# Start addresses of slots, weight units and value tiles, and the job turn of the adaLN sums, in a two-block transformer kernel

## The chip, the cores and the metric

One core of a Trainium2 chip runs the whole program. The metric is the device time of one execution in microseconds (us); three runs of the kernel before were timed.

## The reference

Two blocks work on one sequence of 512 tokens with 1024 features, two layers each, all in float32. A layer of the first block takes a vector `c` to six rows of 1024 numbers, the adaLN shift, scale and gate (`silu(c) @ w_ada + b_ada`), applies them around a mixer (mLSTM heads beside dilated attention) and a SwiGLU, and normalises. The second block does the same with its own adaLN weights, a linear recurrence and stick-breaking attention in its first layer, windowed attention in its second, and a gated feed-forward with a short convolution.

```python
ada = (c_act @ w_ada[l] + b_ada[l])[:, None, :]
sh1, sc1, g1, sh2, sc2, g2 = jnp.split(ada, 6, axis=-1)
u = h * (1.0 + sc1) + sh1
y = mixer(u, w_in[l], ...)                    # u @ w_in, mLSTM, attention, @ w_out
h = layer_norm(DN_ALPHA * h + g1 * y, ...)
u = h * (1.0 + sc2) + sh2
y = (jax.nn.silu(u @ w1) * (u @ w3)) @ w2
```

## The kernel before

**Data.** Activations lie feature by partition: a tile of 128 partitions by 512 tokens in float32 (2048 bytes of each partition) is a *slot*, and there are 60 of them. A product in full precision is made of three fp32r matmuls: each operand is split into a rounded part `h` and a rest `l`, and `h*h`, `l*h` and `h*l` are accumulated in one PSUM tile. Activations are split into two slots; weights stream from HBM in chunks of 16 blocks of 128x128 (`wt`, 1 MB), which ScalarE rounds into `wh` (L517) and VectorE subtracts into `wl` (L520), in *units* of 8 blocks (4096 bytes of each partition; five units of each kind).

**Matmuls.** A matmul has a stationary operand, loaded by a LDWEIGHTS of its own, and a moving operand that streams through. `proj` (L532 to L534) streams 512 tokens of a slot past a block of `wh`, `wh`, `wl`; `proj_halves` (L577, L580, L581) does so with 256 tokens; `fetch`/`begin` (L595 to L597) and `first_block` (L1295 to L1297) are again 512 wide. `proj_tokens` (L553, L556, L557) has it the other way round: a piece of a slot is stationary and 256 columns of `wh` or `wl` are moving. In the mLSTM heads both operands are slots (L889 to L891), and L918 to L920 stream the value tiles `vn0`, `vn1` (258 columns for each of four token groups) past slots. All these are fp32r. Others, L1426 and L714 among them, take plain float32 operands and appear as two records each.

**Addresses.** Pools lie behind each other in SBUF in the order in which they are opened, and a pool's tiles in the order of their first use, each rounded up to 32 bytes: `cp` (constants, columns, `vn`), `wtp` (`wt`), `whp` (units), `adp` (`wada`), `sm` (small columns, each name with 4 buffers unless told otherwise), then `slots`. In the compiled program of before, `vn0` begins at byte 26400 of each partition, `vn1` at 30528, the first unit at 51040 and the first slot at 106400; the rest of units and slots follow in steps of 4096 and 2048. So every slot begins 416 bytes behind a multiple of 512, every unit 352 bytes behind one, and both 32 bytes behind a multiple of 64. A block within a unit and a group of 128 tokens within a slot lie a multiple of 512 bytes further on. The last slot ends 96 bytes below the end of the memory that a partition has.

**adaLN jobs.** `ada` (from L689) is a generator that runs between other work. For each group of 2048 outputs it makes four accumulators: each takes four DMAs of 512 KB (`wada`, on SP's queue, two buffers) and eight VectorE operations (L706 and the line before it). After the first, second and third it yields; after the fourth it goes on at once to four float32 matmuls that add up the 128 partitions of each accumulator (L714) and yields; in its next turn it copies, transposes (L722), adds the bias and yields a last time: five turns for a group. Turns are called by `background()` ahead of a projection: 14 in a mixer (the mixer of layer 0 has two groups to do) and 18 in each feed-forward (three groups, in three of the four); `finish_jobs()` runs what is left. There are 11 groups.

**Order around the start.** `setup` issues the loads of `vecs` (SP) and `cst` (ACT), small memsets on POOL (L642 to L683), and VectorE operations on them, of which L685 fills two columns of each `vn` from a column that POOL has set.

Of the kernel before, what the change touches and what calls it, by code (L numbers as in the profile page):

```python
# [10 lines left out]
F32 = mybir.dt.float32  # L11
F32R = mybir.dt.float32r
# [4 lines left out]
P = 128  # L17
# [434 lines left out]
class Model:  # L452
    def __init__(self, ctx, tc, ins, out, dbg=None, stop=None):
        self.tc, self.nc, self.ins, self.out, self.dbg_out, self.stop = tc, tc.nc, ins, out, dbg, stop
        self.plan = []
        pool = lambda name, bufs, **kw: ctx.enter_context(tc.tile_pool(name=name, bufs=bufs, **kw))
        self.cp = pool("cp", 1)
        self.wtp = pool("wtp", 2)
        self.whp = pool("whp", 5)
        self.adp = pool("adp", 2)  # L460
        self.drp = pool("drp", 2, space=bass.MemoryType.DRAM)
        self.sm = pool("sm", 4)
        self.pacc = pool("pacc", 3, space=PSUM)
        self.pss = pool("pss", 2, space=PSUM)
        self.pst = pool("pst", 1, space=PSUM)
        self.pso = pool("pso", 2, space=PSUM)
        self.slots = pool("slots", 1)
        self.freeq = deque(range(NSLOT))
        self.peak = NSLOT
        self.late = []  # L470
        self.flip = 0
        self.ready = {}
        self.jobs = deque()
        self.later = []


    def get(self, rounded=False):
# [150 lines left out]
    def setup(self):  # L628
        nc = self.nc
        self.vecs = self.cp.tile([P, NVEC], F32, name="vecs")  # L630
        nc.sync.dma_start(out=self.vecs, in_=self.ins["vecs"])
        n = CST["ident"]
        self.sums = self.cp.tile([P, n], F32, name="sums")
        nc.scalar.dma_start(out=self.sums, in_=self.ins["cst"][:, 0:n])
        self.x = [self.get() for _ in range(KD)]
        for k in range(KD):
            (nc.sync if k % 2 else nc.scalar).dma_start(out=self.x[k].f, in_=self.ins["xT"][k])
        self.consts = self.cp.tile([P, NCST - n], F32, name="consts")
        nc.scalar.dma_start(out=self.consts, in_=self.ins["cst"][:, n:])
        self.ident = self.cst("ident")  # L640
        self.eps = self.cp.tile([P, 2], F32, name="eps")
        nc.gpsimd.memset(self.eps[:, 0:1], LN_EPS)  # L642
        nc.gpsimd.memset(self.eps[:, 1:2], RMS_EPS)
        zero = self.cp.tile([P, 1], F32, name="zero")
        nc.gpsimd.memset(zero, 0.0)
        self.zero = zero.to_broadcast([P, T])
        self.mhalf = self.cp.tile([P, 4], F32, name="mhalf")
        nc.gpsimd.memset(self.mhalf, -0.5)
        self.ident_r = self.cp.tile([P, 128], F32R, name="ident_r")
        nc.vector.tensor_copy(self.ident_r, self.ident)  # L650
        self.csil = self.cp.tile([P, 16], F32, name="csil")
        c = self.vec("c1", 0, 16)
        th = self.small(16, "th_c")
        nc.scalar.activation(th, c, AF.Tanh, scale=0.5)
        nc.vector.tensor_scalar(out=th, in0=th, scalar1=0.5, scalar2=0.5, op0=ALU.mult, op1=ALU.add)
        nc.vector.tensor_mul(self.csil, th, c)
        self.n2sp = self.softplus_cols()
        self.n4sp = self.cp.tile([P, 4], F32, name="n4sp")
        nc.vector.tensor_scalar(out=self.n4sp, in0=self.n2sp, scalar1=2.0, scalar2=None, op0=ALU.mult)

        for l in range(DEPTH):
            for name, n in ((f"conv_w{l}_0", 96), (f"gn_w{l}", 8), (f"fcw{l}_0", 4 * KF)):
                v = self.vec(name, 0, n)
                nc.vector.tensor_scalar(out=v, in0=v, scalar1=0.5, scalar2=None, op0=ALU.mult)
        for name in ("eba", "ebx"):
            v = self.vec(name, 0, 4)
            nc.vector.tensor_scalar(out=v, in0=v, scalar1=0.5, scalar2=None, op0=ALU.mult)
        for name in ("eqg", "okg"):
            v = self.vec(name)
            nc.vector.tensor_scalar(out=v, in0=v, scalar1=0.125, scalar2=None, op0=ALU.mult)  # L670
        v = self.vec("b_ada0", 8, 8)
        nc.vector.tensor_scalar(out=v, in0=v, scalar1=1.0, scalar2=None, op0=ALU.add)
        self.dup = self.cp.tile([P, 1], F32, name="dup")
        nc.gpsimd.memset(self.dup, 1.0 / 32)
        self.adac = {}
        for blk in range(2):
            for l in range(DEPTH):
                self.adac[blk, l] = self.cp.tile([P, 48], F32, name=f"ada{blk}{l}")

        self.vn = [self.cp.tile([P, 4, 258], F32R, name=f"vn{k}") for k in range(2)]  # L680
        for k in range(2):
            col = self.small(4, "vcol")
            nc.gpsimd.memset(col, (1 - k) / 16.0)  # L683
            for j in (256, 257):
                nc.vector.tensor_copy(self.vn[k][:, :, j], col)  # L685


    def ada(self, blk, l, groups):
        nc = self.nc  # L689
        w = self.ins["ada1" if blk == 0 else "ada2"][l]  # L690
        bias = f"b_ada{l}" if blk == 0 else f"ada_b{l}"
        ad = self.adac[blk, l]
        for g in groups:
            accs = []
            for n in range(4):
                acc = self.get()
                for q in range(4):
                    wt = self.adp.tile([P, 2, T], F32, name="wada")
                    nc.sync.dma_start(out=wt, in_=w[4 * g + n, q])
                    for j in range(2):  # L700
                        k = 2 * q + j
                        c = self.csil[:, 8 * blk + k:8 * blk + k + 1]
                        if k == 0:
                            nc.vector.tensor_scalar(out=acc.f, in0=wt[:, j, :], scalar1=c, scalar2=None, op0=ALU.mult)
                        else:
                            nc.vector.scalar_tensor_tensor(out=acc.f, in0=wt[:, j, :], scalar=c, in1=acc.f,  # L706
                                                           op0=ALU.mult, op1=ALU.add)
                accs.append(acc)
                if n < 3:
                    yield  # L710

            rows = self.pss.tile([P, T], F32, name="s")
            for n, acc in enumerate(accs):
                nc.tensor.matmul(rows[32 * n:32 * n + 32, :], self.cst("ones", 32), acc.f, start=True, stop=True,  # L714
                                 tile_position=(0, 32 * n))
            self.put(accs)
            rs = self.get()
            yield
            nc.scalar.copy(rs.f, rows)
            cols = self.pst.tile([P, T], F32, name="t")  # L720
            for c in range(4):
                nc.tensor.transpose(cols[:, c * P:(c + 1) * P], rs.f[:, c * P:(c + 1) * P], self.ident)  # L722
            c0 = 16 * g
            nc.vector.tensor_tensor(out=ad[:, c0:c0 + 16].rearrange("p (n c) -> p n c", n=4),
                                    in0=cols.rearrange("p (c n e) -> p n c e", c=4, n=4)[:, :, :, 0],
                                    in1=self.vec(bias, c0, 16).rearrange("p (n c) -> p n c", n=4), op=ALU.add)

            sc = ad[:, 8:16] if g == 0 else ad[:, 32:40]
            if g != 1:
                nc.vector.tensor_scalar(out=sc, in0=sc, scalar1=1.0, scalar2=None, op0=ALU.add)  # L730
            if blk == 0 and g != 0:
                gt = ad[:, 16:24] if g == 1 else ad[:, 40:48]
                nc.vector.tensor_scalar(out=gt, in0=gt, scalar1=0.5, scalar2=None, op0=ALU.mult)
            self.put(rs)
            yield
# [51 lines left out]

    def load_rsqrt(self, dep):

        t = self.small(1, "arsd")  # L790
        return self.nc.scalar.activation(t, dep, AF.Abs_reciprocal_sqrt, bias=1.0, scale=0.0)


# [179 lines left out]
    def attention_pair(self, l, sp, u):  # L973
# [62 lines left out]
        o0 = self.pso.tile([P, T], F32, name="o")  # L1036
        o12 = self.pso.tile([P, T], F32, name="o")
        self.lastmm = {}
        ls, mx = self.small(16, "att_l"), self.small(16, "att_m")
        cols = lambda ap, x, i: ap.rearrange("p (x y i) -> p x y i", x=2, y=2)[:, x, :, i]  # L1040
        bts = [self.get(), self.get()]
        for x in range(2):
# [1 line left out]
        for i in (0, 3, 1, 2):  # L1044
# [12 lines left out]
            for x in range(2):  # L1057
# [17 lines left out]
                t = self.pst.tile([P, T], F32, name="t")  # L1075
# [36 lines left out]
        t = self.pst.tile([P, T], F32, name="t")  # L1112
# [646 lines left out]
```

## Time and profile before

| what | value |
|---|---|
| median of three runs | 3487.23 us (3484.3 to 3487.62) |
| the profiled execution's own time | 3485.64 us |
| its span, first to last instruction | 3483.8 us |
| TensorE busy, matmuls | 3407.2 us, 98% |
| VectorE busy | 2146.2 us, 62% |
| ScalarE busy | 1457.3 us, 42% |
| GpSimd busy | 186.7 us, 5% |
| mean granted TensorE clock | 0.993 |
| mean DMA rate | 114 GB/s |

PE is TensorE's matmuls, PEld its weight loads, DVE is VectorE, ACT ScalarE, POOL GpSimd, SP the sync engine that issues most DMAs. The profiled execution lasts 1.84 us longer than its span; it is 1.59 us shorter than the median. The matmul records overlap, since one is still in the array when the next starts: how fast they follow each other is read from their starts, not from their durations.

### The profile page before, as it was taken

How to read it: one execution, taken by the hardware profiler on the slowest of the kernel's cores; microseconds unless marked ns; L12 is line 12 of the kernel's file. 1: busy time of each engine (PE TensorE's matmuls, PEld its weight loads, DVE VectorE, ACT ScalarE, POOL GpSimd, SP SyncE). 2: the span in 40 equal slices, each digit the busy share in tenths (PEclk: the TensorE clock that was granted, in tenths of full speed). 3: DMA queues.
4: the chain of work that ended last, by engine and by line, in shares of the span. 5: the costliest groups of instructions: out<-in, count | busy, mean ns of one | idle time of the engine just before them, and what ended most of it. 6: DMA issues, size and time to landing. Idle time of an engine off the chain costs nothing.

```text
span 3483.8 us, 45252 instructions
## 1 busy us (share of the span) xinstructions
PE 3407.2 (98%) x17777; PEld 2786.8 (80%) x17777; DVE 2146.2 (62%) x4043; ACT 1457.3 (42%) x2558; POOL 186.7 (5%) x252
## 2 busy tenths in 40 slices
PE   7999999999999999999999999989999999999999
PEld 5788777778888888877788888877688888897887
DVE  5875545648663687554535856368888565865353
ACT  4543555225222554355523422246753234753231
POOL 1110110010000011011000000001000000000000
PEclk9999999999999999999999999999999999999999
DMA  5222222635552222222222555211146432122222
GB/s 218 91 78 80 79 79 103 220 119 178 209 184 94 75 89 79 91 73 76 78 103 85 194 186 193 97 67 61 37 140 235 163 115 85 49 73 97 97 97 73
DMA packets 76117, 395.72 MB, mean 114 GB/s; under 512 B 9200, under 2 KB 10480, under 8 KB 42496
## 3 DMA queue, kind: packets, MB, share of 16 engines
q1 hardware_dynamic: 69408, 377.90, 30.5%
q0 software_dynamic: 4480, 12.69, 1.2%
q8 instruction: 140, 2.29, 0.3%
q10 hardware_dynamic: 2016, 2.25, 0.2%
q14 instruction: 73, 0.60, 0.1%
HBM read 390.60 MB, written 2.20 MB: 113 GB/s over the span
## 4 chain that ended last, share of the span: by engine, by line
PE 84%; DVE 7%; ACT 2%; DMA 2%; issue 1%; POOL 0%; DVEq 0%; ACTq 0%; POOLq 0%
PE acc L532 21%; PE acc L534 21%; PE acc L533 21%; PE acc L577 2%; PE acc L580 2%; PE acc L581 2%; DMA wada<-in_ada_dram 1%; PE o L1096 1%; PE o L1511 1%; DVE wl L520 1%; PE s L1060 1%; DVE slot L706 1%; PE acc L553 1%; PE acc L556 1%; PE acc L557 1%
## 5 line engine op out<-in xcount | busy, mean ns | idle before, releaser
L532 PE MATMUL acc<-slot,wh 128*128 128x512 f32 x3461 | 1373.6, 397 | 14.3 <-DVE slot L802 9.0
L534 PE MATMUL acc<-slot,wl 128*128 128x512 f32 x3461 | 1365.4, 394 | 0.0
L533 PE MATMUL acc<-slot,wh 128*128 128x512 f32 x3461 | 1363.5, 394 | 0.0
L517 ACT CAST wh<-wt 128x1024 fp32r<-128x1024 f32 x522 | 547.2, 1049 | 1223.3 <-PE acc L533 1005.3
L520 DVE TENSOR_TENSOR wl<-wt,wh 128x1024 fp32r<-128x1024 f32 x522 | 645.5, 1238 | 529.4 <-ACT wh L517 520.7
L532 PEld LDWEIGHTS acc<-slot,wh 128*128 128x128 f32 x3461 | 652.6, 189 | 164.7 <-ACT wh L517 13.8
L534 PEld LDWEIGHTS acc<-slot,wl 128*128 128x128 f32 x3461 | 652.1, 188 | 144.1 <-issue 4.6
L533 PEld LDWEIGHTS acc<-slot,wh 128*128 128x128 f32 x3461 | 652.6, 189 | 142.6 <-issue 5.1
L706 DVE SCALAR_TENSOR_TENSOR slot<-wada,csil,slot 128x512 f32<-128x512 f32 x308 | 231.9, 753 | 75.3 <-DMA wada<-in_ada_dram 70.0
L577 PE MATMUL acc<-slot,wh 128*128 128x256 f32 x726 | 207.1, 287 | 4.2 <-ACT slot L376 4.2
L580 PE MATMUL acc<-slot,wh 128*128 128x256 f32 x726 | 205.7, 283 | 0.0
L581 PE MATMUL acc<-slot,wl 128*128 128x256 f32 x726 | 204.4, 282 | 0.1
L608 ACT CAST slot<-slot 128x512 fp32r<-128x512 f32 x204 | 125.4, 620 | 182.1 <-DVE slot L1260 52.8
L1194 DVE SCALAR_TENSOR_TENSOR slot<-acc,ada,slot 128x512 f32<-128x512 f32 (+1 forms) x109 | 70.1, 646 | 160.8 <-PE acc L534 120.8
L802 DVE SCALAR_TENSOR_TENSOR slot<-acc,vecs,slot 128x510 f32<-128x510 f32 (+2 forms) x217 | 159.8, 745 | 8.2 <-ACT slot L797 5.6
L609 DVE TENSOR_TENSOR slot<-slot,slot 128x512 fp32r<-128x512 f32 x204 | 144.4, 714 | 32.7 <-ACT slot L608 23.2
L577 PEld LDWEIGHTS acc<-slot,wh 128*128 128x128 f32 x726 | 136.7, 189 | 12.4 <-issue 6.2
L580 PEld LDWEIGHTS acc<-slot,wh 128*128 128x128 f32 x726 | 137.4, 189 | 2.8 <-issue 1.6
L581 PEld LDWEIGHTS acc<-slot,wl 128*128 128x128 f32 x726 | 137.3, 189 | 0.7 <-DVE wl L520 0.3
L553 PE MATMUL acc<-wh,slot 128*128 128x256 f32 x288 | 81.3, 282 | 0.0
L556 PE MATMUL acc<-wh,slot 128*128 128x256 f32 x288 | 81.2, 282 | 0.0
L557 PE MATMUL acc<-wl,slot 128*128 128x256 f32 x288 | 80.7, 280 | 0.0
(357 smaller groups left out, 3931.4 us busy)
## 6 DMA issues: line engine op xcount, KB each, us to landing
wt<-in_ws_dram SPq DMA_DIRECT2D x261, 1024.0 KB, 4.8
wada<-in_ada_dram SPq DMA_DIRECT2D x176, 512.0 KB, 4.5
slot<-in_ada_dram SPq DMA_DIRECT2D x32, 256.0 KB, 6.1
slot<-drc POOLq DMA_DIRECT2D x16, 256.0 KB, 3.6
slot<-in_bias_dram POOLq DMA_DIRECT2D x16, 256.0 KB, 2.9
slot<-dr POOLq DMA_DIRECT2D x32, 128.0 KB, 3.1
out_dram<-slot SPq DMA_DIRECT2D x8, 256.0 KB, 2.0
slot<-in_xT_dram ACTq DMA_DIRECT2D x4, 256.0 KB, 5.6
```

Of the source, the lines that this page charges most:

```text
L517: copy = nc.scalar.copy(self.wh, src)
L520: nc.vector.tensor_tensor(out=self.wl, in0=src, in1=self.wh, op=ALU.subtract)
L532: nc.tensor.matmul(acc, wh, xs[k].h.r, start=k == 0, stop=False)
L533: nc.tensor.matmul(acc, wh, xs[k].l.r, start=False, stop=False)
L534: nc.tensor.matmul(acc, wl, xs[k].h.r, start=False, stop=k == n - 1)
L577: m = nc.tensor.matmul(acc[:, hs], wh, xs[k].h.r[:, hs], start=k == 0, stop=False)
L580: nc.tensor.matmul(acc[:, hs], wh, xs[k].l.r[:, hs], start=False, stop=False)
L581: last[a] = nc.tensor.matmul(acc[:, hs], wl, xs[k].h.r[:, hs], start=False, stop=k == n - 1)
L608: copy = self.nc.scalar.copy(pair.h.r, src)
L609: self.nc.vector.tensor_tensor(out=pair.l.r, in0=src, in1=pair.h.f, op=ALU.subtract)
L706: nc.vector.scalar_tensor_tensor(out=acc.f, in0=wt[:, j, :], scalar=c, in1=acc.f, op0=ALU.mult, op1=ALU.add)
L802: nc.vector.scalar_tensor_tensor(out=out[:, lo:hi], in0=acc[:, lo + d:hi + d], scalar=w, in1=out[:, lo:hi], op0=ALU.mult, op1=ALU.add)
```

## The change

A new method `pad(pool, n)` allocates a tile of `n` bytes and sets its first element with a POOL memset. It is called five times, ahead of `sums`, ahead of `ident_r`, ahead of each `vn` tile (32 bytes each) and behind the second (96 bytes). Small tiles that had four buffers get one (`th_c`, `vcol`, `arsd`) or two (`att_l`, `att_m`). By the sizes of the tiles, `vn0` then begins at byte 26496 and `vn1` at 30656 (multiples of 64), the first unit at 51264 (64 bytes behind a multiple of 512) and the first slot at 105984 (a multiple of 512). In `ada` the generator yields after the fourth accumulator too: the four matmuls of L714 go out one turn later, and a group takes six turns.

```diff
+    def pad(self, pool, n):
+        self.pads += 1
+        t = pool.tile([P, n // 4], F32, name=f"pad{self.pads}", tag=f"pad{self.pads}", bufs=1)
+        self.nc.gpsimd.memset(t[:, 0:1], 0.0)
...
+        self.pad(self.cp, 32)
         self.sums = self.cp.tile([P, n], F32, name="sums")
...
+        self.pad(self.cp, 32)
         self.ident_r = self.cp.tile([P, 128], F32R, name="ident_r")
...
-        th = self.small(16, "th_c")
+        th = self.small(16, "th_c", 1)
...
-        self.vn = [self.cp.tile([P, 4, 258], F32R, name=f"vn{k}") for k in range(2)]
+        self.vn = []
         for k in range(2):
-            col = self.small(4, "vcol")
+            self.pad(self.cp, 32)
+            self.vn.append(self.cp.tile([P, 4, 258], F32R, name=f"vn{k}"))
+        self.pad(self.cp, 96)
+        for k in range(2):
+            col = self.small(4, "vcol", 1)
...
                 accs.append(acc)
-                if n < 3:
-                    yield
+                yield
...
-        t = self.small(1, "arsd")
+        t = self.small(1, "arsd", 1)
...
-        ls, mx = self.small(16, "att_l"), self.small(16, "att_m")
+        ls, mx = self.small(16, "att_l", 2), self.small(16, "att_m", 2)
```

## Rows read from the trace of the kernel before

**Rows 1.** The chain of waits: shares of the span by engine, then by line.

```profile
PE 84%; DVE 7%; ACT 2%; DMA 2%; issue 1%; POOL 0%; DVEq 0%; ACTq 0%; POOLq 0%
...
by line: PE acc L532 21.4%; PE acc L534 21.3%; PE acc L533 21.2%; PE acc L577 1.7%; PE acc L580 1.6%; PE acc L581 1.6%; DMA wada<-in_ada_dram 1.3%; PE o L1096 1.0%; PE o L1511 0.9%; issue 0.9%; DVE wl L520 0.9%; PE s L1060 0.8%; DVE slot L7
```

**Rows 2.** Stretches: length, busy us by engine (x count), PE clock, DMA share, GB/s.

```profile
3200.00:3300.00 100.00, 100.00 (x438) 82.07 (x437) 41.71 (x47) 27.03 (x31) 0.00 (x0) 1.00 0.27 95
```

**Rows 3.** Timeline of PE, L532 to L534, first and last of 714: start, duration.

```profile
1724.91 0.39 PE L534 MATMUL acc<-slot,wl 128*128 128x512 f32 x1
...
1888.11 0.39 PE L534 MATMUL acc<-slot,wl 128*128 128x512 f32 x1
```

**Rows 4.** Timeline of PE, L889 to L891, first and last of 12.

```profile
277.39 0.39 PE L889 MATMUL s<-slot,slot 128*128 128x512 f32 x1
...
279.88 0.39 PE L891 MATMUL s<-slot,slot 128*128 128x512 f32 x1
```

**Rows 5.** Timeline of PE, L577 to L581: ends of 120 matmuls, then of 190.

```profile
769.19 0.28 PE L577 MATMUL acc<-slot,wh 128*128 128x256 f32 x1
...
782.67 0.28 PE L581 MATMUL o<-slot,wl 128*128 128x256 f32 x1
...
809.04 0.28 PE L581 MATMUL acc<-slot,wl 128*128 128x256 f32 x1
...
831.30 0.28 PE L581 MATMUL o<-slot,wl 128*128 128x256 f32 x1
```

**Rows 6.** Timeline of PE, L553 to L557: ends of 91 matmuls, then of 96.

```profile
148.71 0.28 PE L557 MATMUL acc<-wl,slot 128*128 128x256 f32 x1
...
158.91 0.28 PE L557 MATMUL acc<-wl,slot 128*128 128x256 f32 x1
...
266.08 0.28 PE L553 MATMUL acc<-wh,slot 128*128 128x256 f32 x1
...
277.27 0.28 PE L557 MATMUL acc<-wl,slot 128*128 128x256 f32 x1
```

**Rows 7.** Timeline of PE, L532 to L534 near the start, first and last of 11.

```profile
104.58 0.40 PE L534 MATMUL acc<-slot,wl 128*128 128x512 f32 x1
...
106.91 0.39 PE L532 MATMUL acc<-slot,wh 128*128 128x512 f32 x1
```

**Rows 8.** Groups by line and shape: count, busy us, mean ns, idle before; PE's timeline, L1426.

```profile
L532 PE MATMUL acc<-slot,wh 128*128 128x512 f32 x3461 | 1373.6, 397 | 14.3 <-DVE slot L802 9.0 <-DVE slot L1259 3.3 <-ACT slot L608 1.1
...
L577 PE MATMUL acc<-slot,wh 128*128 128x256 f32 x726 | 207.1, 287 | 4.2 <-ACT slot L376 4.2
...
L553 PE MATMUL acc<-wh,slot 128*128 128x256 f32 x288 | 81.3, 282 | 0.0
...
L577 PE MATMUL o<-slot,wh 128*128 128x256 f32 x224 | 63.2, 282 | 0.0
...
L1426 PE MATMUL s<-slot,slot 128*128 128x512 f32 x16 | 7.5, 592 | 0.0
...
2356.04 1.88 PE L1426 MATMUL s<-slot,slot 128*128 128x512 f32 x4
```

**Rows 9.** Groups by line: adaLN's VectorE operations and the four sums.

```profile
L706 DVE SCALAR_TENSOR_TENSOR slot<-wada,csil,slot 128x512 f32<-128x512 f32 x308 | 231.9, 753 | 75.3 <-DMA wada<-in_ada_dram 70.0
...
L714 PE MATMUL s<-slot,sums 128*32 128x512 f32 x88 | 17.9, 605 | 5.9 <-DVE slot L706 5.9
```

**Rows 10.** Timeline of the start, POOL and DVE; idle time before in brackets.

```profile
0.90 0.13 POOL L683 MEMSET vcol<- 128x4 f32 x2
1.03 0.38 DVE L685 CAST vn<-vcol 128x4 fp32r<-128x4 f32 x4 [1.03 <-POOL vcol L683]
...
4.46 0.71 DVE L664 TENSOR_SCALAR vecs<-vecs 128x96 f32<-128x96 f32 x6 [3.04 <-DMA vecs<-in_vecs_dram]
```

**Rows 11.** Stretches with the most VectorE work, columns as in rows 2.

```profile
800.00:900.00 100.00, 98.64 (x557) 83.46 (x557) 85.10 (x133) 41.67 (x64) 0.00 (x0) 1.00 0.62 216
...
2600.00:2700.00 100.00, 100.00 (x441) 81.18 (x440) 85.52 (x119) 35.34 (x45) 0.00 (x0) 1.00 0.67 237
```

More of the change, by code (lines that the diff above doesn't have):

```diff
@@ L474, in __init__ @@
         self.later = []
+        self.pads = 0
+    def pad(self, pool, n):
+        self.pads += 1
+        t = pool.tile([P, n // 4], F32, name=f"pad{self.pads}", tag=f"pad{self.pads}", bufs=1)
+        self.nc.gpsimd.memset(t[:, 0:1], 0.0)
     def get(self, rounded=False):
```

## The prediction

> **What bounds the kernel now.** I read the chain of waits first: TensorE's matmuls hold 84% of it, and three lines, L532 to L534, hold 21.4 + 21.3 + 21.2 = 63.9% [rows 1], 2226 us of the span of 3483.8. L577, L580 and L581 hold another 4.9%, 171 us. Then the stretches: where nothing but 512-wide matmuls runs, 438 start in 100 us at a granted clock of 1.00, the level of 2.4 GHz [rows 2]. So the question is what sets the distance between two starts, the pitch.
>
> Timelines give it closely. L532 to L534 make 713 steps in 163.20 us: 228.9 ns, or 549.3 ticks of 2.4 GHz for 512 columns [rows 3]. That is 37.3 ticks over one column a tick (213.3 ns), 112 in three matmuls. L889 to L891, as wide, make 11 steps in 2.49 us, 226.4 ns, about 32 ticks over [rows 4]. The 256-wide lines run at either of two pitches: L577 to L581 at 13.48 us / 119 = 113.3 ns in one stretch and 22.26 us / 189 = 117.8 ns in another [rows 5], L553 to L557 at 10.20 / 90 = 113.3 and 11.19 / 95 = 117.8 [rows 6]. Against 106.7 ns that is 16 and 26.7 ticks over, 48 or 80 in three matmuls. Near the start, L532 to L534 even show 2.33 us / 10 = 233 ns, 48 ticks over [rows 7]. Every excess, over three matmuls, is a multiple of 16 ticks, and 16 columns of float32 are 64 bytes of a partition.
>
> So I read the excess as 64-byte pieces (6.67 ns each) that the moving operand reads, or waits for, beyond its own. The moving operands of all these lines begin 32 bytes behind a multiple of 64: they touch 33 pieces where 32 would hold the data, or 17 where 16 would. That is one extra piece in each matmul, and the whole excess of the faster 256-wide stretches. The rest, 1.33 pieces in L532 to L534, one in L889 to L891, none or 0.67 in the 256-wide lines, goes with the relation of the two operands: the weights begin 64 bytes below the moving operand (modulo 512) in L532 and L577, at the same place in L889, 64 above it in L553. I take it for meetings with the weight load that runs beside each matmul. With the weights above, six of L553's nine stretches run at the faster pitch; with the weights below, two of the ten long stretches (over 100 steps) of L577 do.
>
> **The change part by part.** *Addresses.* Slots move to multiples of 512 and units 64 bytes above: moving operands begin on a piece, a weight block fills 8 pieces instead of touching 9, and in L532 and L577 the weights come to lie 64 bytes above the moving operand, the relation that L553 has now (L553 takes the opposite one). No fp32r row has a start at a multiple of 64 with 256 or 512 columns, so the pitch is bounded from both sides: 228.9 ns if nothing changes, 213.3 if every column takes its tick and nothing else. Plain float32 matmuls, which move half a column a tick, show what is left where reading does not bind: four records of L1426 take 1.88 us and one takes 0.592, so they step at 1.288 / 3 = 429.3 ns, 2.6 over the 426.7 of 1024 ticks [rows 8]. I take that: 215.9 for 512 columns and 109.3 for 256. Both sources of excess are then gone; the second, because L553's faster stretches show it at zero under the relation that comes.
> - 512 wide: 2226 us / 228.9 ns = 9725 matmuls on the path, x 13.0 ns = 126.4 us.
> - 256 wide: 171 us / 117.3 ns (mostly the slower pitch) = 1458, x 8.0 = 11.7 us. L553 to L557 (3 x 288, [rows 8]), on average (6 x 113.3 + 3 x 117.8) / 9 = 114.8, x 5.5 = 4.8 us.
> - Were every matmul counted, on the path or not (3 x 3461 and 3 x (726 + 224), [rows 8]): 10383 x 13.0 + 2850 x 8.0 + 4.8 = 163 us. With nothing changed: 0.
>
> L532 and L889, both 512 wide at the same start, step differently [rows 3, 4], so the weight load seems to cost reading time. "TensorE: Matmul & The Clock Gate", section "Step-by-step: what each phase is for", of the Trainium skill says that the engine reads moving operand and weights through two independent ports and that loading the next weights takes nothing from the running matmul. By that rule only the extra piece could go, and the sum would be that of rival 1; by the rows it is the one above.
>
> The value tiles (480 matmuls of L918 to L920) have 258 columns, 1032 bytes, which touch 17 pieces from either start: 0, with bounds of 3 us either way (480 x 6.67). Whether VectorE, ScalarE or DMAs work faster or slower at the new addresses no row shows. They hold 11% of the chain; 2% of that is 8 us either way, and I take 0.
>
> *The four sums, a turn later.* PE waited 5.9 us in all for the last L706 ahead of L714 [rows 9]. One turn later, the eight VectorE operations (8 x 0.75 = 6 us) have a projection's time to finish, at least 24 matmuls or 5.2 us and mostly twice that. Of 5.9 us I take 4; bounds 0 and 12, twice the row, for the loads that wait along with their matmuls. The count of DMAs and operations stays. What moves: each later group's `wada` loads stand a turn or two further back in SP's queue, among the same `wt` loads; the first group's keep their place. 18 turns hold three groups of six exactly, and 14 hold two; every column set is first read after its feed-forward or mixer, so no consumer comes closer than that.
>
> *Small edits.* Five POOL memsets of 0.1 us, and one wait: the second `vcol` memset must follow the first casts of L685, and a cast then waits for it. Both lie in the 3.04 us in which VectorE waits for `vecs` [rows 10]; without that cover they would cost some 0.5 us. `att_l` and `att_m` with two buffers are reused two pairs later, after their readers have finished. `arsd` is never read.
>
> Sum: 126.4 + 11.7 + 4.8 + 4 = 146.9 us off the profiled execution's own 3485.64: 3338.7; the median stands 1.6 us above that execution, so 3340. What is late next is VectorE: in the busiest stretches it has 85 us of work in 100 [rows 11], and 100 us shrink to some 94, so there it stays below TensorE. Where PE waits for it today, the chain's shares already leave the matmuls out.
>
> **The rivals.**
> 1. *Only the extra piece goes.* Weight loads meet the moving reads as before. For: L577 reaches 113.3 with today's relation too, so how a stretch began counts as well as the relation. Against: L553. Gain 6.67 ns x (9725 + 1458 + 864) = 80.4, plus 4: 3401, the median 3403.
> 2. *The start does not matter.* The excess is the rate of fp32r reads, and a start at a multiple of 32 is as good as any. For: no row shows a better start. Against: several pitches at one width. Then only L714's 4 us come: 3481.6, the median 3483, which is no change. "SBUF — State Buffer", section "Specifications (TRN2)", of the Trainium skill gives lines of 16 bytes; every start before is a multiple of 32 already, and by that rule no pitch moves.
> 3. *Slower: the weight load falls in step with the moving reads.* Both now begin on pieces, and a read that is held back by one piece may meet the next weight piece too. Place: every matmul of L532 to L534. It decides from 34.33 - 32 = 2.33 lost pieces a matmul on; a weight block has 8. At three, the pitch is 233.3 ns: 9725 x 4.4 + 1458 x 9.4 + 864 x 11.9 = 67 us more, less 4: 3548.3, the median 3550. For: 233 ns occur [rows 7]. Against: they are rare, and no long 256-wide stretch exceeds 117.8 in either relation.
>
> **How the numbers follow.** Forecast 0.55, rival 1 0.25, rival 2 0.12, rival 3 0.08. A measurement of this kernel can tell about 0.2%, 7 us, from no change. Faster by more: 0.80; within: 0.12; slower: 0.08. The range leaves out rivals 2 and 3, 0.20 in all. Its low end takes every matmul, all 12 us of L714 and the two unknowns of 3 and 8 us: 3485.6 - 163 - 12 - 11 = 3300. Its high end lies behind rival 1, for stretches that settle at a slower pitch while VectorE takes over some of the path: 3450.
>
> **What would show it.** Right: starts of L532 to L534 at 214 to 217 ns, some 463 in a 100 us stretch without other matmuls instead of 438; L577 at 110 or less; L714 without idle time ahead of it; VectorE's busy time unchanged at a higher share. At 222 ns rival 1 holds, at 228.9 rival 2, at 233 or more rival 3. If the pitch falls and the span does not, I have missed what is late next: then PE's idle time ahead of L532, 14.3 us now [rows 8], will have grown, and the chain names VectorE.

## The result, and the profile after

The changed kernel takes 3516.93 us (median of four runs, 3514.03 to 3522.94) where the kernel before takes 3487.43 beside it: a ratio of 1.009, with a 95% interval of 1.0078 to 1.0102. It is 29.5 us slower, where the forecast was 147 us faster. The profiled execution took 3522.94 us with a span of 3521.2, 37.3 us over the profiled execution of before. One execution of the last kernel below, `same_place_old_turn`, ran at a mean granted clock of 0.509 and took 11865.05 us; its median is that of the other five.

The changed kernel has more lines, so the same code stands elsewhere: L532, L533, L534 are now L540, L541, L542; L577, L580, L581 are L585, L588, L589; L553, L556, L557 are L561, L564, L565; L889 to L891 are L902 to L904; L706 and L714 are L720 and L727.

The page's busy line and the chain of waits of the changed kernel, by engine and by line:

```profile
PE 3446.3 (98%) x17777; PEld 2781.0 (79%) x17777; DVE 2150.9 (61%) x4043; ACT 1458.0 (41%) x2558; POOL 187.1 (5%) x257
...
PE 85%; DVE 7%; ACT 2%; DMA 1%; issue 1%; POOL 0%; DVEq 0%; ACTq 0%; POOLq 0%
PE acc L540 22%; PE acc L541 22%; PE acc L542 22%; PE acc L585 2%; PE acc L588 1%; PE acc L589 1%; PE o L1109 1%; DVE wl L528 1%; PE o L1524 1%; PE s L1073 1%; PE acc L561 1%; PE acc L564 1%; PE acc L565 1%; DVE slot L375 1%; DVE slot L377 1%
```

The chain has the shape of [rows 1]: the same three lines hold two thirds. TensorE's instructions are as many as before and its busy time is 39 us longer; VectorE and ScalarE have 2150.9 and 1458.0 us of work (2146.2 and 1457.3 before). So no other engine became slower; the matmuls did. The three stretches of [rows 2] and [rows 11] (length, busy us by engine with counts, granted clock, DMA share, GB/s):

```profile
3200.00:3300.00 100.00, 100.00 (x430) 80.60 (x429) 47.17 (x57) 31.06 (x38) 0.00 (x0) 1.00 0.27 95
...
800.00:900.00 100.00, 97.73 (x559) 82.97 (x558) 82.95 (x132) 43.05 (x67) 0.00 (x0) 0.98 0.56 200
...
2600.00:2700.00 100.00, 98.33 (x486) 79.97 (x485) 86.86 (x126) 40.18 (x53) 0.00 (x0) 1.00 0.63 218
```

The first is the one to compare, since it holds 512-wide matmuls alone in both kernels: 430 start in 100 us instead of 438, at a granted clock of 1.00 as before, the level of 2.4 GHz. (The other two now hold another mix of widths.) Two matmuls stand further apart. TensorE's timeline, start and duration, first and last of four long runs of equal steps:

```profile
283.87 0.39 PE L902 MATMUL s<-slot,slot 128*128 128x512 f32 x1
...
286.40 0.39 PE L904 MATMUL s<-slot,slot 128*128 128x512 f32 x1
...
268.41 0.28 PE L561 MATMUL acc<-wh,slot 128*128 128x256 f32 x1
...
279.60 0.28 PE L565 MATMUL acc<-wl,slot 128*128 128x256 f32 x1
...
773.09 0.28 PE L585 MATMUL acc<-slot,wh 128*128 128x256 f32 x1
...
786.58 0.28 PE L589 MATMUL o<-slot,wl 128*128 128x256 f32 x1
...
1741.51 0.40 PE L540 MATMUL acc<-slot,wh 128*128 128x512 f32 x1
...
1907.65 0.39 PE L542 MATMUL acc<-slot,wl 128*128 128x512 f32 x1
```

- L540 to L542: 712 steps in 166.14 us, 233.3 ns, where [rows 3] have 228.9. All 17 stretches of more than 160 matmuls step so.
- L585 to L589: 119 steps in 13.49 us, 113.4 ns, the faster of the two pitches of [rows 5]. Over all regular steps of these lines the mean falls from 117.3 to 114.2.
- L561 to L565: 95 steps in 11.19 us, 117.8 ns, the slower one of [rows 6]; the mean rises from 114.9 to 117.8.
- L902 to L904: 11 steps in 2.53 us, 230.0 ns (226.4 in [rows 4]). Their distance is 0 in both kernels. It is the heads of these short stretches that became longer: the steps come down to 226 or 227 ns with the last two here, and within the first three or so in the stretches of 12 before.

No line went below the lowest pitch that its width had before. Heads aside, the lines exchanged pitches among those that had been there.

Groups by line and shape (count, busy us, mean ns, idle before and what ended it):

```profile
L540 PE MATMUL acc<-slot,wh 128*128 128x512 f32 x3461 | 1383.9, 400 | 16.6 <-DVE slot L815 9.5 <-DVE slot L1272 4.8 <-ACT slot L826 1.2
L720 DVE SCALAR_TENSOR_TENSOR slot<-wada,csil,slot 128x512 f32<-128x512 f32 x308 | 233.0, 756 | 52.9 <-DMA wada<-in_ada_dram 47.1
...
L727 PE MATMUL s<-slot,sums 128*32 128x512 f32 x88 | 16.9, 605 | 2.0 <-DVE slot L720 2.0
```

PE's idle time ahead of L540 is 16.6 us, 14.3 for L532 in [rows 8]: nothing else has taken the path. The four sums wait 2.0 us instead of 5.9 [rows 9], and VectorE's waits for `wada` fall from 70.0 to 47.1 us. The start, VectorE's timeline with the idle time before in brackets:

```profile
1.19 0.24 DVE L699 CAST vn<-vcol 128x4 fp32r<-128x4 f32 x2 [1.19 <-POOL vcol L697]
1.69 0.24 DVE L699 CAST vn<-vcol 128x4 fp32r<-128x4 f32 x2 [0.26 <-POOL vcol L697]
4.40 0.71 DVE L674 TENSOR_SCALAR vecs<-vecs 128x96 f32<-128x96 f32 x6 [2.47 <-DMA vecs<-in_vecs_dram]
```

The single `vcol` splits the casts into two pairs, with 0.26 us between them, and `vecs` still ends the wait after them: the small edits cost nothing, as foreseen with [rows 10].

### The profile page after: what moved, and what is told of

Its sections match the earlier page's. It is cut to its first block, busy times and chain, and to the rows that moved or that the text cites. A ratio compares the mean times of both kernels' runs of the same rounds, so it can differ in the third digit from the quotient of the medians.

```text
span 3521.2 us, 45287 instructions
## 1 busy us (share of the span) xinstructions
PE 3446.3 (98%) x17777; PEld 2781.0 (79%) x17777; DVE 2150.9 (61%) x4043; ACT 1458.0 (41%) x2558; POOL 187.1 (5%) x257
## 4 chain that ended last, share of the span: by engine, by line
PE 85%; DVE 7%; ACT 2%; DMA 1%; issue 1%; POOL 0%; DVEq 0%; ACTq 0%; POOLq 0%
PE acc L540 22%; PE acc L541 22%; PE acc L542 22%; PE acc L585 2%; PE acc L588 1%; PE acc L589 1%; PE o L1109 1%; DVE wl L528 1%; PE o L1524 1%; PE s L1073 1%; PE acc L561 1%; PE acc L564 1%; PE acc L565 1%; DVE slot L375 1%; DVE slot L377 1%
## 5 line engine op out<-in xcount | busy, mean ns | idle before, releaser
L540 PE MATMUL acc<-slot,wh 128*128 128x512 f32 x3461 | 1383.9, 400 | 16.6 <-DVE slot L815 9.5
L541 PE MATMUL acc<-slot,wh 128*128 128x512 f32 x3461 | 1378.5, 398 | 0.0
L542 PE MATMUL acc<-slot,wl 128*128 128x512 f32 x3461 | 1375.3, 397 | 0.0
L540 PEld LDWEIGHTS acc<-slot,wh 128*128 128x128 f32 x3461 | 652.0, 188 | 183.6 <-ACT wh L525 11.0
L542 PEld LDWEIGHTS acc<-slot,wl 128*128 128x128 f32 x3461 | 652.2, 188 | 157.3 <-issue 4.1
L541 PEld LDWEIGHTS acc<-slot,wh 128*128 128x128 f32 x3461 | 652.2, 188 | 156.9 <-issue 6.2
L720 DVE SCALAR_TENSOR_TENSOR slot<-wada,csil,slot 128x512 f32<-128x512 f32 x308 | 233.0, 756 | 52.9 <-DMA wada<-in_ada_dram 47.1
L585 PE MATMUL acc<-slot,wh 128*128 128x256 f32 x726 | 205.9, 285 | 4.7 <-ACT slot L376 4.3
L588 PE MATMUL acc<-slot,wh 128*128 128x256 f32 x726 | 204.5, 282 | 0.0
L589 PE MATMUL acc<-slot,wl 128*128 128x256 f32 x726 | 203.2, 280 | 0.2 <-DVE wl L528 0.2
L585 PEld LDWEIGHTS acc<-slot,wh 128*128 128x128 f32 x726 | 137.1, 190 | 13.2 <-issue 6.2
L588 PEld LDWEIGHTS acc<-slot,wh 128*128 128x128 f32 x726 | 137.9, 190 | 2.8 <-issue 1.6
L589 PEld LDWEIGHTS acc<-slot,wl 128*128 128x128 f32 x726 | 137.8, 190 | 0.7 <-DVE wl L528 0.4
L561 PE MATMUL acc<-wh,slot 128*128 128x256 f32 x288 | 81.9, 284 | 0.0
L564 PE MATMUL acc<-wh,slot 128*128 128x256 f32 x288 | 81.6, 283 | 0.0
L565 PE MATMUL acc<-wl,slot 128*128 128x256 f32 x288 | 81.1, 282 | 0.0
```

The source lines that it names most:

```text
L540: nc.tensor.matmul(acc, wh, xs[k].h.r, start=k == 0, stop=False)
L541: nc.tensor.matmul(acc, wh, xs[k].l.r, start=False, stop=False)
L542: nc.tensor.matmul(acc, wl, xs[k].h.r, start=False, stop=k == n - 1)
L585: m = nc.tensor.matmul(acc[:, hs], wh, xs[k].h.r[:, hs], start=k == 0, stop=False)
L588: nc.tensor.matmul(acc[:, hs], wh, xs[k].l.r[:, hs], start=False, stop=False)
L589: last[a] = nc.tensor.matmul(acc[:, hs], wl, xs[k].h.r[:, hs], start=False, stop=k == n - 1)
```

## The experiments

Two theories stood at first. One: a later start of the moving operand did give its piece back, and something else took more. The other: the start at a multiple of 64 does nothing, and the distance from the moving operand to the weights, modulo 512, sets the pitch alone. "Distance" below is the address of the weights minus that of the moving operand; it was -64 in L532 and L577 and +64 in L553, and the change exchanges the two signs.

**A table of pitches.** 48 matmuls a stretch, in the threes of L532, two stretches for each start, distance and width. One of the two (`stall`) stands behind a break: three or four matmuls of another stretch, or idle time. The other (`flow`) mostly follows the stretch before it directly:

```diff
+            a = m // 4 + (512 if i % 3 == 1 else 0)
+            b = w0 + 128 * (2 * (i // 3 % 8) + (1 if i % 3 == 2 else 0))
+            nc.tensor.matmul(acc[:, 0:n], wts[:, b:b + 128], mov[:, a:a + n], start=i == 0, stop=i == COUNT - 1)
```

> Computes none of the reference; it only times matmuls: 128 stretches of 48 fp32r matmuls (two of three with the same kind of operand order as in the model), 512 or 256 columns wide, the moving operand at byte 0 or 32 of a multiple of 512, the weights at d = -256 to 224 bytes from it in steps of 32 (modulo 512); once with a stop before each stretch, once without. Theory A (the relation of the two operands sets the pitch): at the same d the two starts give the same pitch; for 512 columns d = -64 gives 228.9 ns, d = 0 226.7, d = 64 233.3, for 256 columns 117.8 (or 113.3), 117, 113.3. Theory B (the start itself does): start 0 and start 32 differ by about 4 ns at every d, and d matters little. If an offset exists that is free of meetings, A expects 220 ns or less at some d.

The timeline shows each stretch as one row (start, duration of all 48, and the distance behind the d of its name); here are three distances at 512 columns, with the moving operand first at start 0, then at start 32:

```profile
632.60 11.16 PE L39 MATMUL flow_n_m_d-64x<-mov,wts 128*128 128x512 f32 x48
...
654.80 11.05 PE L39 MATMUL flow_n_m_d0x<-mov,wts 128*128 128x512 f32 x48
...
676.88 11.36 PE L39 MATMUL flow_n_m_d64x<-mov,wts 128*128 128x512 f32 x48
...
810.77 11.16 PE L39 MATMUL flow_n_m_d-64x<-mov,wts 128*128 128x512 f32 x48
...
832.97 11.05 PE L39 MATMUL flow_n_m_d0x<-mov,wts 128*128 128x512 f32 x48
...
855.04 11.36 PE L39 MATMUL flow_n_m_d64x<-mov,wts 128*128 128x512 f32 x48
```

In these undisturbed stretches starts at 0 and 32 gave the same pitch at every distance (at four distances the 512-wide stretches of start 0 all stand behind breaks; past their first steps they agree too), and the distance counts modulo 256. At 512 columns, from the first start to the last: 226.7 ns at distance 0, 229.0 at -64, 233.4 at 64, and between 232.5 and 234.2 at the other multiples of 32. At 256 columns: 119.9 at 0 and 117.8 at -64. At 64 two pitches occur: 117.8 in the four stretches without a break, 113.3 in three of the four behind one, once their first steps are past. The start falls out, the distance stays; and the distance that is best at 256 columns is not the best at 512.

**The change taken apart.** The turn alone, the addresses alone, and the addresses of before with nothing moved but the units, by 128 bytes, so that the distance becomes +64 while every start stays 32 bytes behind a multiple of 64.

The first is against the kernel before, the second against the changed kernel, the third against the kernel before (the smaller tiles make the room that the pad takes, so that the slots stay where they are modulo 512):

```diff
-                if n < 3:
-                    yield
+                yield
```

```diff
-                yield
+                if n < 3:
+                    yield
```

```diff
+        pad = self.cp.tile([P, 32], F32, name="pad")
+        nc.gpsimd.memset(pad[:, 0:1], 0.0)
...
-        ls, mx = self.small(16, "att_l"), self.small(16, "att_m")
+        ls, mx = self.small(16, "att_l", 2), self.small(16, "att_m", 2)
```

> The kernel before with the four sums a turn later and no address moved. Theory A: L714 loses its 5.9 us of waits, 3481 to 3485 us. Rival C (the turn is what costs): 3510 us or more.

> The changed kernel with the sums in their old turn. Theory A: 10,400 matmuls of 512 columns at 233.3 instead of 228.9 ns (+46), 2850 of 256 at some 114.2 instead of 117.3 (-9), 864 at 117.8 instead of 114.8 (+3): 40 us slower than before, 3520 to 3530 us. Rival C: 3490 us or less.

> The kernel before with the units alone moved by 128 bytes, so that they lie 64 bytes above the slots (modulo 512) as in the changed kernel, but every slot still begins 32 bytes behind a multiple of 64. Theory A: L532 to L534 at 233.3 ns, L577 at 113.3 to 114.5, 3515 to 3530 us. Theory B: 228.9 ns and 117.3 as before, 3487 us.

The turn alone: 3481.35 against 3488.81, ratio 0.9983 (0.9974 to 0.9993). The addresses alone: 3521.57, ratio 1.010 (1.0086 to 1.0113). The units moved alone: 3522.24, ratio 1.0103 (1.0087 to 1.0118). The long stretch of `units_up_64` (timeline of TensorE, first and last of 713):

```profile
1742.28 0.40 PE L532 MATMUL acc<-slot,wh 128*128 128x512 f32 x1
...
1908.41 0.40 PE L534 MATMUL acc<-slot,wl 128*128 128x512 f32 x1
```

166.13 us / 712 = 233.3 ns, the pitch of the changed kernel to a tenth, with starts as before. Its 256-wide lines stand at 115.0 and 117.8 ns on average, near the changed kernel's 114.2 and 117.8. Even L889 to L891, whose own start and distance are those of before, step at 231.0 ns on average (228.3 before, 230.5 in the changed kernel): their short stretches depend on what runs ahead of them. So the whole loss comes from the distance, and neither the pieces nor the starts have a part in it. The wait of the four sums, first in `turn_only`, then in `addresses_only` (groups by line):

```profile
L713 PE MATMUL s<-slot,sums 128*32 128x512 f32 x88 | 16.9, 605 | 1.1 <-DVE slot L706 1.1
```

```profile
L728 PE MATMUL s<-slot,sums 128*32 128x512 f32 x88 | 17.9, 605 | 4.3 <-DVE slot L720 4.3
```

The turn does what it says, with either set of addresses.

**Finer steps, other starts, fewer weight columns.** To find whether any address reaches one column a tick, and what fewer weight columns do:

```diff
+        for d in range(0, 256, 8):
+            stretch(f"step{n}d{d}", n, 0, d)
+        for m in (4, 16, 32, 48):
+            stretch(f"start{n}m{m}", n, m, 0)
...
+        for w in (32, 64, 96):
+            for d in (0, 64, 192):
+                stretch(f"cols{n}w{w}d{d}", n, 0, d, None, None, w)
```

> Computes none of the reference; it only times matmuls, 48 in a stretch, 512 or 256 columns wide: (step) the weights 0 to 248 bytes above the moving operand in steps of 8; (start) the moving operand at 4, 16, 32 or 48 bytes behind a multiple of 512, weights at the same place; (two) the third weight block of each three at another distance than the first two; (low) the second moving operand at another start than the first; (cols) 32, 64 or 96 weight columns instead of 128. Theory A: (start) all give 226.7 ns (512) as at 0. If the excess comes from meetings with the weight load, fewer weight columns give a lower pitch, down to 220 ns or less at 32 columns; if it is the rate of fp32r reads, it stays at 226 or more. (step): pieces of 64 bytes mean plateaus or a slope between the values at 0, 32 and 64 (226.7, 233.3, 233.3); a better distance than 0 would show below 226.7.

The timeline shows each stretch as one row: start, duration of all 48, and in the name the columns, the distance d (192 is -64), the start m and the weight columns w. The last matmul lasts 0.39 us (0.28 at 256 columns), so the mean pitch is the duration less that, over 47:

```profile
102.58 11.36 PE L38 MATMUL step512d64x<-mov,wts 128*128 128x512 f32 x48
...
281.07 11.15 PE L38 MATMUL step512d192x<-mov,wts 128*128 128x512 f32 x48
...
369.86 11.56 PE L38 MATMUL start512m4x<-mov,wts 128*128 128x512 f32 x48
381.26 11.21 PE L38 MATMUL start512m16x<-mov,wts 128*128 128x512 f32 x48
392.31 11.09 PE L38 MATMUL start512m32x<-mov,wts 128*128 128x512 f32 x48
...
414.27 11.06 PE L38 MATMUL two512d0e0x<-mov,wts 128*128 128x512 f32 x48
...
614.02 11.27 PE L38 MATMUL cols512w32d0x<-mov,wts 128*32 128x512 f32 x48
625.13 11.28 PE L38 MATMUL cols512w32d64x<-mov,wts 128*32 128x512 f32 x48
...
647.37 11.21 PE L38 MATMUL cols512w64d0x<-mov,wts 128*64 128x512 f32 x48
...
713.79 5.90 PE L38 MATMUL step256d0x<-mov,wts 128*128 128x256 f32 x48
...
759.29 5.62 PE L38 MATMUL step256d64x<-mov,wts 128*128 128x256 f32 x48
...
1035.83 5.60 PE L38 MATMUL cols256w64d0x<-mov,wts 128*64 128x256 f32 x48
...
1046.71 5.61 PE L38 MATMUL cols256w64d192x<-mov,wts 128*64 128x256 f32 x48
```

At distance 64: (11.36 - 0.39) / 47 = 233.4 ns. At -64: 228.9. At 0: 227.0 from start 0 (`two512d0e0`) and 227.7 from start 32, the same within a step or two at the head of a stretch; 230.2 from start 16 and 237.7 from start 4. At 256 columns distance 0 gives 119.6 and distance 64 gives 113.6, here without a break ahead; so a break is not what decides between the two pitches of that distance. At 512 columns starts off the multiples of 32 do cost, and from one multiple of 32 to another nothing changes. No distance in steps of 8 bytes went below 226.6 ns, nor did the stretches of this run (not shown) in which a second distance or a second start is mixed in.

Fewer weight columns act differently at the two widths. At 512 columns they bring no gain over 227.0: at distance 0, 64 of them take 230.2 ns and 32 take 231.5. At 256 columns they do: with 64 or 32 of them each of the three distances steps at 113.2 to 113.4 ns, where 128 take 119.6 at distance 0. And with 32 the distance no longer matters at either width: at 512 columns distance 64 takes 231.7, beside 231.5 at 0. So in this run the effect of the distance hangs on the number of weight columns, which speaks for my word "meetings", but something else holds up the pitch at 512 columns. The output has fewer rows too when the weights have fewer columns, and no run tells the two apart.

**The two operands at the same place, and the old distance from the new starts.** Both against the changed kernel. First `same_place`, with units and slots at multiples of 512; then `minus_64`, with the units there and the slots 64 bytes behind:

```diff
-        self.pad(self.cp, 96)
+        self.pad(self.cp, 32)
+        self.pad(self.sm, 64)
```

```diff
-        self.pad(self.cp, 96)
+        self.pad(self.cp, 32)
+        self.pad(self.sm, 128)
```

> The changed kernel with the units at the same place as the slots, both at multiples of 512 (distance 0 in place of 64). Theory A by the table of pitches: 10,400 matmuls at 226.7 instead of 228.9 ns (-23), 2850 of 256 columns at 120 instead of 117.3 (+8), 864 at 120 instead of 114.8 (+4), the turn -6: 3468 to 3476 us, faster than both. Theory B (the 64-byte start costs): 3500 us or more.

> The changed kernel with units at multiples of 512 and slots 64 bytes behind one: the distance of before, -64, but with every start on a multiple of 64. Theory A: 228.9 ns at L540 to L542 and the time of the turn alone, 3478 to 3486 us. Theory B: 3510 us or more.

`same_place`: 3472.88 against 3486.51, ratio 0.9956 (0.9942 to 0.997). `minus_64`, every start a multiple of 64 and the distance that of before: 3478.76, ratio 0.9977 (0.9967 to 0.9986), which is `turn_only` within the intervals. The long stretches, first of `same_place` (712 steps), then of `minus_64` (713):

```profile
1718.31 0.40 PE L540 MATMUL acc<-slot,wh 128*128 128x512 f32 x1
...
1879.71 0.39 PE L542 MATMUL acc<-slot,wl 128*128 128x512 f32 x1
```

```profile
1716.06 0.39 PE L542 MATMUL acc<-slot,wl 128*128 128x512 f32 x1
...
1879.27 0.39 PE L542 MATMUL acc<-slot,wl 128*128 128x512 f32 x1
```

161.40 us / 712 = 226.7 ns and 163.21 / 713 = 228.9 ns: what the table has for distances 0 and -64, to 0.1 ns. The second is the pitch of [rows 3] to a tenth, from starts at a multiple of 64: the start at a multiple of 64 is worth nothing. At distance 0 the 256-wide lines step at 119.8 ns on average, worse than before, and the kernel gains all the same, since it has more than three times as many regular 512-wide steps (some 9800 in L540 to L542 against some 2700 in L577's place).

**Without the turn.** `same_place` with the old turn, to see whether its gain is the addresses' own:

```diff
-                yield
+                if n < 3:
+                    yield
```

> Units and slots at the same place (distance 0), the four sums in their old turn. Theory A: the addresses alone give -10 to -14 us by the table of pitches, 3474 to 3480 us, so that the turn and the addresses add up to the time of the run with both. If the turn's gain were part of the addresses', this run would equal the one with both, 3473 us.

3473.38 against 3485.80, ratio 0.9962 (0.9949 to 0.9975), just below the 3474 to 3480 us expected. The addresses carry nearly all of it: the median with the turn is 0.5 us lower, far within the intervals, so that these two runs can't show what the turn adds. The sums wait 6.3 us without it, 3.2 with it:

```profile
L729 PE MATMUL s<-slot,sums 128*32 128x512 f32 x88 | 18.0, 605 | 6.3 <-DVE slot L721 6.3
```

**Other widths, and bfloat16 beside them.** What is left over one column a tick, by width; `half` is the same stretch with bfloat16 operands:

```diff
+    for n in (128, 192, 256, 320, 384, 448, 512):
+        for d in (0, 64, 128, 192):
+            stretch(f"wide{n}d{d}", n, 0, d)
+    for n in (512, 256, 128):
+        half(n)
```

> Computes none of the reference; it only times matmuls, 48 in a stretch: fp32r with 128 to 512 columns in steps of 64, weights 0, 64, 128 or 192 bytes above the moving operand, and bf16 with 512, 256 and 128 columns at one place. Theory A1 (fp32r itself streams a column in 17/16 of a tick, 34 pieces of time for 512 columns and 17 for 256, and meetings come on top): the lowest pitch at every width is N x 0.4427 ns (56.7, 85.0, 113.3, 141.7, 170.0, 198.3, 226.7), and bf16 goes below it, to 216 ns at 512. Theory A2 (one extra piece of 6.67 ns per matmul, whatever the width): the lowest pitch is (N + 16) / 2.4, 60.0, 86.7, 113.3, 140.0, 166.7, 193.3, 220.0, and 220 does not occur only because of meetings.

The timeline again, a row for each stretch:

```profile
22.30 10.44 PE L43 MATMUL wide128d64x<-mov,wts 128*128 128x128 f32 x48
32.54 10.44 PE L43 MATMUL wide128d128x<-mov,wts 128*128 128x128 f32 x48
...
99.92 7.20 PE L43 MATMUL wide320d0x<-mov,wts 128*128 128x320 f32 x48
106.96 7.21 PE L43 MATMUL wide320d64x<-mov,wts 128*128 128x320 f32 x48
...
190.90 9.76 PE L43 MATMUL wide448d192x<-mov,wts 128*128 128x448 f32 x48
200.50 11.04 PE L43 MATMUL wide512d0x<-mov,wts 128*128 128x512 f32 x48
211.37 11.36 PE L43 MATMUL wide512d64x<-mov,wts 128*128 128x512 f32 x48
...
244.74 10.53 PE L51 MATMUL bf512x<-bm,bw 128*128 128x512 bf16 x48
255.11 5.40 PE L51 MATMUL bf256x<-bm,bw 128*128 128x256 bf16 x48
```

From the start of one stretch to the start of the next are 48 steps: bfloat16 steps at 10.37 / 48 = 216.0 ns at 512 columns, fp32r at 10.87 / 48 = 226.5 at best. In units of 6.67 ns, the lowest pitches of fp32r are 22 for 320 columns (7.04 / 48 = 146.7 ns), 30 for 448 (9.60 / 48 = 200.0) and 34 for 512: two over the 20, 28 and 32 of one column a tick; 384 columns (173.3) are two over as well. At 256 columns it is one over, the 17 of [rows 5], and 192 (111.7) and 128 (213.3) are far over. So neither a share of the columns nor one piece for each matmul fits all widths, and where the excess comes from stays open. The distance has a different effect at each width too: at 320 and 128 columns none beyond 0.2 ns (one stretch aside, the first of all), at 448 the best is -64 (200.0, and 202.9 at 0), at 512 it is 0.

## Why the prediction was wrong

**What bounds the kernel** was read rightly: the pitch of 512-wide fp32r matmuls sets the time, and the number of them on the path (9725) was right enough to price its change. 9725 x 4.4 ns = 42.8 us lost, 1458 x 3.1 = 4.5 gained in L585 to L589, 864 x 2.9 = 2.5 lost in L561 to L565, some 4 gained by the turn: 36.8 us in sum, beside 37.3 between the profiled executions and 29.5 between the medians.

**The step that failed** is the sentence "Both sources of excess are then gone; the second, because L553's faster stretches show it at zero under the relation that comes." It has two errors.

The second source first, since it made the loss. L553's stretches have 256 columns, and I carried their best distance to 512 columns. There the order is another: 0 is best, -64 costs 2.2 ns more and +64 6.6. The term of 126.4 us gained became some 43 lost. The one row that showed 512 columns at another distance was L889 to L891, at distance 0 and 226.4 ns [rows 4]. It was read as one piece left to lose; it was the best pitch that this width has at any address tried. In the kernel the distance would have had to go from -64 to 0, as in `same_place`, not to +64.

The first source was no source. The 33rd piece of a start at 32 was a figure for which each measured excess, a multiple of 16 ticks, seemed to speak, but every moving operand of 256 or 512 columns began at such a start, so none of the rows used could tell a piece too many from a fixed cost. `minus_64` and the tables tell them apart: the start is worth nothing, and what I took for the extra piece is there from every start. The estimate of 215.9 ns was taken from plain float32 for want of a nearer row; it fits bfloat16, and no fp32r stretch came near it.

**Term by term.** 512 wide: 126.4 us gained foreseen, 42.8 lost. 256 wide: 11.7 foreseen, 4.5 gained by the relation alone: L585 now stays mostly at the faster of its old pitches, as L553 did. L561: 4.8 gained foreseen, 2.5 lost, as it takes the relation that L577 had. The four sums: 4 us foreseen; 3.9 us of PE's wait are gone in the changed kernel, and the turn alone takes 0.17% off, 5.9 us (2.4 to 9.1 by its interval). Value tiles, VectorE, ScalarE, DMAs and the small edits: 0 foreseen, and no row shows otherwise.

**The rivals.** Rival 3 gave the pitch, 233.3 ns, and the sign, but its mechanism fails: two operands that both begin on pieces should have cost a third piece, and `units_up_64` has the same pitch from starts off the pieces. The third piece should have slowed the 256-wide lines too, to 126.7 ns, and L585 became faster. That is most of why the time is 3517 and not 3550. The match of the pitch is luck, as far as the runs show. Its evidence against, "they are rare", was the weak place: [rows 7] had the 233 ns for 512 columns, and I set them aside. Rival 2 was right on the start: with the old distance, as in `minus_64`, new starts bring nothing beyond the turn. But it took it that nothing else moves the pitch.

The case for two sources rested on the weight load taking reading time. The Trainium skill, "TensorE: Matmul & The Clock Gate", section "Step-by-step: what each phase is for", has the two operands read through independent ports, so that the next load takes no reading bandwidth from the running matmul. The tables do not agree that the operands are without effect on each other: with everything else the same, the place of the weights alone moves the pitch from 226.7 to 233.4 ns at 512 columns, and with 32 weight columns that effect is gone. They do not show that it is the load's reading, since at 512 columns no smaller load went below 227 ns.

## What to carry to other kernels

Before an operand is moved, measure the pitch at the width that carries the time, over the distance between the two operands and over the start, each by itself; a few dozen matmuls a stretch suffice. A relation read at one width is no evidence for another, and a fixed cost that every row shares can't be split from a cost of alignment when all rows have one alignment. Of the three distances tried in this kernel, 0 (weights and moving operand at the same address modulo 256) is the best for 512-wide fp32r matmuls, and with it the kernel beats both others though it is the worst of the three for 256 columns.

## What was not expected of the hardware

- The pitch of fp32r matmuls depends on the distance of the weights from the moving operand modulo 256 bytes, by 226.7 to 234.3 ns at 512 columns and 113.3 to 120.0 at 256 (multiples of 32), and the two orders differ.
- At one distance there can be two pitches. At 256 columns both 113.3 and 117.8 ns occur at 64 and at -64; in the kernels no stretch of 60 or more of the main lines changes its pitch once its first steps are past, though the first 192-wide stretch of `pitch_widths` goes from 213 to 112 ns on its way. In the profiled execution of `turn_only`, all long stretches but the last step at 228.9 ns, as in [rows 3]; the last, at the same distance, runs its whole length at 344.86 us / 1478 = 233.3 ns:

```profile
3138.74 0.40 PE L532 MATMUL acc<-slot,wh 128*128 128x512 f32 x1
...
3483.60 0.39 PE L534 MATMUL acc<-slot,wl 128*128 128x512 f32 x1
```

That is 1478 x 4.4 = 6.5 us, most of the 8.2 by which this execution (3489.54) lies above its median. The kernel before began the same stretch after the same wait of 2.05 us, its first matmuls 0.43 us apart as here, and then stepped at 228.9; so neither of these decides, and what does is open. [rows 7], with 233 ns at distance -64, may be another such case, but 11 matmuls are too few to tell it from a slow head.

- fp32r pays at least 13.2 ns a matmul over one column a tick at 512 columns, bfloat16 2.7. The Trainium skill, "TensorE: Matmul & The Clock Gate", section "Wait — 56ns, not 53.3ns?", states a floor of about 2.5 ns for each matmul and 215.7 ns at 512 columns; the bfloat16 rows here agree within 0.3 ns, and the fp32r rows at 512 columns lie 10.8 ns above it or more.
- At 128 columns fp32r matmuls step at 10.24 / 48 = 213.3 ns, as long as 512 columns would take at one a tick.
